# Adding x in the output stage by an accumulating transfer, behind a copy by ScalarE

## The chip, the cores and the metric

The kernel runs on one core of a Trainium2 chip. The metric is the time of one execution on the device in microseconds (us); three runs of the kernel before stand for its time. Engines are named as in the profile: PE is TensorE's matrix multiplication and PEld its weight load, DVE is VectorE, ACT is ScalarE, POOL is GpSimd, SP is SyncE. A name with a q is that engine's sequencer, which also issues transfers (SPq, POOLq).

## The reference

One layer of a trunk: an RMS norm, a pooling mixer whose branch is gated, a residual addition and a final RMS norm, on x of 4096 rows and 1024 columns in float32.

```python
normed = rms_norm(x, norm_w)
u, gate = split(normed @ in_w, 2)               # 1024 -> 2048
pooled = trailing means of u over 2/4/8/16 rows - u
y = (pooled @ group_w + group_b) * scale * silu(gate)
h = x + y @ out_w                               # the output stage: 1024 -> 1024
out = rms_norm(h, final_w)
```

## The kernel before

The products are done in float32 with two parts: a number is split into a rounded high part and a rest (`split`, L167 to L170: ScalarE copies the high part, VectorE subtracts for the rest), and each product is three matmuls (`mm3`). On top of that every large product is cut into 2 x 2 quarters and done with seven products, P1 to P7, in place of eight (a Strassen-Winograd scheme).

There are three stages in the list `steps` (L1069): "a" and "b" compute the gate and the pooled branch in blocks of 1024 rows and store the gated branch as `yd`; "o", the output stage, multiplies it by out_w, adds x and normalizes. The output stage starts near 615 us of the span and takes 8 blocks of 512 rows.

A block of the output stage has 256 rows in "half 1" (the first ones) and 256 in "half 0". Each half is held as two row tiles j = 0 and 1 of 128 rows and 1024 columns, `hs[b][half, j]`, and each row tile has two column halves n = 0 and 1 of 512. The order of the products is P1, P7, P6, P2, P5, P4, P3 (`ORDER_OUT`). Four pairs of PSUM banks rotate from block to block: x, v, y and spare. What is done behind each product, in `evict_o`:

- P1 fills the pair x, and ScalarE copies it into y as the start of P6 (L1023).
- P7 fills v; it is added into half 1, n = 1. P6 adds to y; y is added into half 1, n = 0.
- P2 adds to x; x is added into half 0, n = 0.
- P5 adds to y; y is added into half 1, n = 1. P4 adds to v; v is added into half 1, n = 0; half 1 is complete, and `finish` normalizes and stores it.
- P3 adds to y; y is added into half 0, n = 1; half 0 is complete.

All these additions are VectorE's (L1033), of 128 x 512 from a bank, into row tiles that hold x already: `load_h` (L852) takes a row tile and lets SyncE load x into it, 512 KB each, four products ahead of use.

From block 2 on, P2 is itself cut into seven inner products of half the size ("inner blocks"). P2, P3 and P4 go to the banks x[0] and x[1], P1 and P7 to spare[0] and spare[1] (`product_inner`, L701). `add_inner` (L711) adds 128 columns of a spare bank into a row tile of half 0. The inner P6 and P5 add on to spare[0] during and after the outer P5:

```python
            if j == 1 and inner and i == P5:     # between the two rows of the outer P5
                product_inner(P6)
                add_inner(0, (1, 0))
                add_inner(1, (1, 0), (1, 1))
...
        elif inner and i == P5:                  # behind the outer P5
            product_inner(P5)
            add_inner(0, (0, 1), (1, 1))
```

So spare[0] is read three times, and each inner product that adds on to it has to wait until the reading before it is done. `add_inner(0, (0, 0))`, the first reading, stands at the head of P2's eviction (L1013).

The order of instructions on an engine follows the program, except where the framework's scheduler takes one that is ready earlier; each engine then works its list in that order, and waits are semaphores that the framework sets from the tiles that an instruction reads and writes. A transfer waits on the queue of the engine that issues it. Transfers of the output stage are all on SyncE (x, yd, out); GpSimd only does the small arithmetic of the inverse root in `finish` (L207 to L225).

## Time and profile before

| | us |
|---|---|
| median of 3 runs | 911.19 (911.1 to 911.32) |
| span of the profiled execution, first to last instruction | 909.7 |
| PE busy | 900.6 |
| DVE busy | 764.5 |
| ACT busy | 461.8 |
| POOL busy | 49.9 |

The page gives no time of the profiled execution beside its span; the median of the runs is 1.5 us longer. In rows of a timeline the columns are start, duration, engine, line, operation, written tile <- read tile, shapes and count; brackets hold the idle time of the engine before the row and what ended it. In rows of groups the figures behind the bar are busy time, mean duration in ns, and idle time with its releasers.

### The profile page before, as it was taken

To read this page: it belongs to the slowest core of one execution; us is meant where nothing else is said; L and a number is where in the kernel's file an instruction comes from. 1 tells how busy PE (TensorE), PEld (TensorE's weight loads), DVE (VectorE), ACT (ScalarE), POOL (GpSimd) and SP (SyncE) were. 2 spreads that over 40 slices of the span, in tenths; PEclk is the share of its full clock that TensorE was granted. 3 is DMA by queue.
4 is the path that set the end of the run, shared out by engine and by line. 5 is a ranking of instruction groups with operands and counts; after the bars stand their busy time and mean duration, and the time that the engine had idled before them with its cause. 6 is when DMAs were issued, how large, how long until landed. Compare 5 with 4: busy or idle time off the path is not lost.

```text
span 909.7 us, 11455 instructions
## 1 busy us (share of the span) xinstructions
PE 900.6 (99%) x4320; PEld 790.1 (87%) x4320; DVE 764.5 (84%) x909; ACT 461.8 (51%) x693; POOL 49.9 (5%) x124
## 2 busy tenths in 40 slices
PE   9999999999999999999999999999999999999997
PEld 7888888888888888888888888888888898888886
DVE  3889995985995997696798699699989878978886
ACT  7869547547446565355445545644424424335334
POOL 0020100100110000000000000000201001001000
PEclk9999999999999999999999999999999999999998
DMA  9977766577675454116616714636385464464332
GB/s 341 401 291 240 276 235 230 189 270 253 217 272 196 156 202 145 47 64 212 255 47 234 275 70 158 235 105 219 137 280 181 149 226 155 146 232 139 116 139 93
DMA packets 66807, 178.08 MB, mean 196 GB/s; under 512 B 6080, under 2 KB 23872, under 8 KB 66752
## 3 DMA queue, kind: packets, MB, share of 16 engines
q1 hardware_dynamic: 60176, 155.83, 48.8%
q0 software_dynamic: 5856, 20.46, 6.1%
q10 hardware_dynamic: 720, 1.06, 0.3%
q8 instruction: 34, 0.56, 0.2%
q14 instruction: 21, 0.17, 0.1%
HBM read 116.50 MB, written 60.83 MB: 195 GB/s over the span
## 4 chain that ended last, share of the span: by engine, by line
PE 91%; DMA 4%; DVE 3%; issue 1%; ACT 0%; SPq 0%; POOL 0%; DVEq 0%; ACTq 0%; POOLq 0%
PE bank L603 88%; PE bank L701 3%; DMA early<-in_wut 2%; DMA st<-in_x 1%; DMA vt<-yd 1%; DVE vt L1033 1%; PE bank L406 1%; DVE op L159 1%; DVE st L159 0%; DVE vt L916 0%; ACT st L943 0%; DVE vt L162 0%; DVE vt L711 0%; SPq L370 0%; DVE st L1033 0%
## 5 line engine op out<-in xcount | busy, mean ns | idle before, releaser
L603 PE MATMUL bank<-op,w 128*128 128x512 f32 x2688 | 580.9, 379 | 0.0
L603 PEld LDWEIGHTS bank<-op,w 128*128 128x128 f32 x2688 | 508.5, 189 | 71.8 <-ACT bank L165 0.4
L603 PE MATMUL bank<-w,op 128*128 128x512 f32 (+1 forms) x1212 | 262.2, 377 | 0.0
L603 PEld LDWEIGHTS bank<-w,op 128*128 128x128 f32 x1212 | 226.3, 189 | 30.7
L165 ACT ACTIVATE op<-st 128x1024 fp32r<-128x1024 f32 x129 | 134.7, 1053 | 142.2 <-PE bank L603 90.5
L159 DVE TENSOR_TENSOR op<-st,op 128x1024 fp32r<-128x1024 f32 x129 | 156.8, 1222 | 51.7 <-ACT op L165 51.3
L156 DVE TENSOR_TENSOR vt<-vt 128x1024 f32<-128x1024 f32 (+6 forms) x72 | 88.2, 1236 | 0.6
L159 DVE TENSOR_TENSOR op<-vt,op 128x1024 fp32r<-128x1024 f32 x43 | 52.5, 1222 | 19.8 <-ACT op L165 19.6
L165 ACT ACTIVATE vt<-bank 128x512 f32<-128x512 f32 x82 | 47.6, 593 | 41.4 <-PE bank L603 40.5
L165 ACT ACTIVATE op<-vt 128x1024 fp32r<-128x1024 f32 x43 | 45.1, 1053 | 39.3 <-PE bank L603 30.2
L159 DVE TENSOR_TENSOR st<-st,st 128x1024 f32<-128x1024 f32 (+1 forms) x43 | 47.0, 1111 | 2.3 <-ACT st L912 1.3
L165 ACT ACTIVATE bank<-bank 128x512 f32<-128x512 f32 x48 | 27.9, 581 | 32.9 <-PE bank L603 32.9
L1033 DVE TENSOR_TENSOR vt<-bank,vt 128x512 f32<-128x512 f32 (+1 forms) x55 | 37.1, 677 | 7.4 <-PE bank L603 7.0
L165 ACT ACTIVATE st<-bank 128x512 f32<-128x512 f32 x48 | 27.8, 593 | 28.7 <-PE bank L603 22.3
L207 POOL TENSOR_SCALAR oms<-oss 128x2 f32<-128x2 f32 x14 | 8.4, 601 | 565.5 <-ACT st L912 460.6
L159 DVE TENSOR_TENSOR w<-st,w 128x1024 fp32r<-128x1024 f32 x25 | 30.2, 1223 | 7.8 <-ACT w L165 7.8
L165 ACT ACTIVATE w<-st 128x1024 fp32r<-128x1024 f32 x25 | 26.0, 1052 | 14.2 <-PE bank L603 9.6
L788 DVE SCALAR_TENSOR_TENSOR st<-vt,colt,st 128x512 f32<-128x512 f32 x46 | 32.7, 752 | 0.1
L1033 DVE TENSOR_TENSOR st<-bank,st 128x512 f32<-128x512 f32 x42 | 28.8, 692 | 3.9 <-PE bank L603 3.7
L783 DVE SCALAR_TENSOR_TENSOR vt<-vt,vt 128x1024 f32<-128x1024 f32 x24 | 29.4, 1227 | 0.3
L916 DVE SCALAR_TENSOR_TENSOR vt<-vt,ors,st 128x1024 f32<-128x1024 f32 x18 | 22.5, 1282 | 7.9 <-POOL ors L225 7.9
L165 ACT ACTIVATE st<-st 128x1024 f32<-128x1024 f32 x16 | 16.9, 1059 | 21.8 <-DVE st L156 21.7
(132 smaller groups left out, 619.0 us busy)
## 6 DMA issues: line engine op xcount, KB each, us to landing
st<-in_x SPq DMA_DIRECT2D x30, 512.0 KB, 5.3
st<-in_xt SPq DMA_DIRECT2D x28, 512.0 KB, 5.6
sd<-st POOLq DMA_DIRECT2D x28, 512.0 KB, 4.6
vt<-in_x SPq DMA_DIRECT2D x27, 512.0 KB, 4.5
st<-sd SPq DMA_DIRECT2D x24, 512.0 KB, 4.2
yd<-st SPq DMA_DIRECT2D x23, 512.0 KB, 2.6
st<-yd SPq DMA_DIRECT2D x20, 512.0 KB, 4.6
out<-vt SPq DMA_DIRECT2D x18, 512.0 KB, 3.6
```

Source lines behind the costliest of these rows:

```text
L156: nc.vector.tensor_tensor(out=dst, in0=a, in1=b, op=ALU.add)
L159: return nc.vector.tensor_tensor(out=dst, in0=a, in1=b, op=ALU.subtract)
L165: return nc.scalar.activation(dst, src, func)
L207: (nc.vector if on_vector and not first else nc.gpsimd).tensor_scalar(out=ms, in0=ss, scalar1=1.0 / D, scalar2=EPS, op0=ALU.mult, op1=ALU.add)
L406: latest[0] = nc.tensor.matmul(ps, a[:, kk, 2 * j + t, :], maps, start=t + m == 0, stop=t == 1 and m == len(pairs) - 1,).ins
L603: latest[0] = nc.tensor.matmul(ps, a, b, start=start and n == 0, stop=stop and n == 2, skip_group_check=True).ins
L701: latest[0] = nc.tensor.matmul(ps, x1, x2, start=i in (P1, P7) and k + n == 0, stop=k == 1 and n == 2, skip_group_check=True,).ins
L783: nc.vector.scalar_tensor_tensor(out=s[:, :, at : at + H], in0=s[:, :, at : at + H], scalar=1.0 / win, in1=v[:, :, HIST:], op0=ALU.mult, o ...
L788: nc.vector.scalar_tensor_tensor(out=sg[:, j], in0=s[:, j, at : at + H], scalar=bias_c[2 * grp + j], in1=sg[:, j], op0=ALU.add, op1=ALU.mult,)
L916: nc.vector.scalar_tensor_tensor(out=us[j], in0=us[j], scalar=rs[:, j : j + 1], in1=fw[0], op0=ALU.mult, op1=ALU.mult,)
L1033: partial["added"] = nc.vector.tensor_tensor(out=dst, in0=src, in1=dst, op=ALU.add).ins
```

## The change

In blocks 0 to 6 the first bank that goes to a part of a row tile (P7, P6, P2) is no longer added to x by VectorE; ScalarE copies it, and x is added to the row tile behind it by a transfer on GpSimd's queue that accumulates into SBUF. Half 1 gets x for all columns behind P6, half 0 for the left columns behind P2; the right columns of half 0 (P3) are still loaded ahead by SyncE, 256 KB a row tile, and added by VectorE. `add_inner(0, (0, 0))` moves behind P2's copies. The last block loads and adds as before.

```diff
     def load_h(b, half):
         for j in range(2):
             u = take("p (a b) -> p a b", a=2)
-            r = b * TO + (1 - half) * TH + j * P
-            nc.sync.dma_start(out=u.rearrange("p a b -> p (a b)"), in_=x[r : r + P, :])
+            if b == NBO - 1:
+                nc.sync.dma_start(
+                    out=u.rearrange("p a b -> p (a b)"), in_=x[row_of(b, half, j), :]
+                )
+            elif half == 0:
+                nc.sync.dma_start(out=u[:, 1], in_=x[row_of(b, half, j), H:])
             hs[b][half, j] = u
+
+    def add_h(b, half, cols):
+
+        for j in range(2):
+            u = hs[b][half, j].rearrange("p a b -> p (a b)")
+            nc.gpsimd.dma_start(
+                out=u[:, cols], in_=x[row_of(b, half, j), cols], accum_op=ALU.add
+            )
...
         if inner and i == P2:
             inner["rows"] = [hs[b][0, j][:, 0] for j in range(2)]
-            add_inner(0, (0, 0))
...
             u = hs[b][half, j][:, n]
+            if not final and i in (P7, P6, P2):
+                copy(halved(u), plain(ps[j]))
+                continue
             last = final and i in (P4, P3)
...
+        if inner and i == P2:
+            add_inner(0, (0, 0))
+        if not final and i == P6:
+            add_h(b, 1, slice(0, D))
+        elif not final and i == P2:
+            add_h(b, 0, slice(0, H))
         if final and i == P3:
```

## The prediction

> **What bounds the kernel now.** The page comes first, for the span and the engines' shares.

> ```profile
> span 909.7 us, 11455 instructions
> PE 900.6 (99%) x4320; PEld 790.1 (87%) x4320; DVE 764.5 (84%) x909; ACT 461.8 (51%) x693; POOL 49.9 (5%) x124
> PE 91%; DMA 4%; DVE 3%; issue 1%; ACT 0%; SPq 0%; POOL 0%; DVEq 0%; ACTq 0%; POOLq 0%
> ```

> TensorE is busy for 99% and holds 91% of the chain that ended last. The runs shown have a median of 911.19 us, so 1.5 us lie around the span; the sums below are changes to the span, and I add them to the median. Next the stage that is changed, by the table of windows (columns: PE, PEld, DVE, ACT, POOL busy, granted clock, DMA share, GB/s).

> ```profile
> 700.00:740.00 40.00, 40.00 (x212) 35.65 (x211) 35.10 (x47) 15.49 (x21) 1.93 (x10) 1.00 0.67 228
> 740.00:780.00 40.00, 40.00 (x217) 35.93 (x216) 34.20 (x44) 15.38 (x21) 3.30 (x10) 1.00 0.40 141
> 820.00:860.00 40.00, 39.74 (x207) 35.16 (x206) 33.97 (x46) 16.18 (x22) 3.02 (x10) 1.00 0.42 145
> ```

> TensorE has no idle time in two of them and 0.26 us in the third, at clock 1.00. VectorE is at 85 to 88%, ScalarE at 39%. Taking work from VectorE can therefore win only what TensorE loses to VectorE. Since a busy PE can hide short waits, I looked for them in the timeline of each inner block (2 to 6), at the weight loads.

> ```profile
> 708.84 0.75 PEld L701 LDWEIGHTS bank<-inner,op 128*128 128x128 f32 x6 [0.19 <-DVE vt L711]
> ...
> 780.52 0.74 PEld L701 LDWEIGHTS bank<-inner,op 128*128 128x128 f32 x6 [0.28 <-DVE vt L711]
> ...
> 849.79 0.68 DVE L1033 TENSOR_TENSOR st<-bank,st 128x512 f32<-128x512 f32 x1
> ...
> 851.52 0.69 DVE L1033 TENSOR_TENSOR vt<-bank,vt 128x512 f32<-128x512 f32 x1
> ...
> 852.12 0.42 DVE L711 TENSOR_TENSOR vt<-bank,vt 128x256 f32<-128x256 f32 x1
> 852.59 0.74 PEld L701 LDWEIGHTS bank<-inner,op 128*128 128x128 f32 x6 [0.67 <-DVE vt L711]
> ```

> In blocks 2, 4 and 6 the inner P6 writes spare bank 0 before VectorE has read it in `add_inner(0, (0, 0))`. The three waits make 0.19 + 0.28 + 0.67 = 1.14 us. The tail holds nothing for this change:

> ```profile
> 889.30 2.61 PE bank L603 x12
> 891.93 0.69 DVE vt L1033
> ```

> VectorE takes up the chain at 891.93 right behind a matmul of the last block, so it arrives there without a backlog, and the last block is unchanged.

> **The change part by part.** It touches blocks 0 to 6.

> ```profile
> L165 ACT ACTIVATE st<-bank 128x512 f32<-128x512 f32 x48 | 27.8, 593 | 28.7 <-PE bank L603 22.3
> ...
> L1033 DVE TENSOR_TENSOR vt<-bank,vt 128x512 f32<-128x512 f32 x53 | 36.2, 687 | 7.4 <-PE bank L603 7.0
> ```

> *Removed from VectorE:* 6 additions a block at 0.687 us, 4.1 us a block, 28.9 us in all. *Added to ScalarE:* 6 copies a block at 0.593 us, 3.6 us a block; its 15.4 of 40 us becomes about 19.4. Both lie beside TensorE. On the path they are worth at most the 1.14 us. In block 6, two additions that go (849.79 and 851.52, 0.6 us of the stream each) stand shortly before the 852.12 one, so it starts about 1.2 us earlier against a wait of 0.67; blocks 2 and 4 waited less. I take the whole 1.14 us.

> *Loads on SyncE:* four x loads of 512 KB a block become two of 256 KB (right half of half 0). The view of SyncE's waits shows what they held up:

> ```profile
> SPq L856 <- DVE op L159: 37.6, 11, 7.9
> ```

> For 37.6 us the queue stood at such a load until a slot was free. Fewer loads waiting for a slot let the yd loads behind them go earlier. No such landing ends a TensorE wait except through the 0.67 already counted, so I book nothing. The wait for a free slot moves to ScalarE's first copy; the x load into the same slot used to be issued long before that point, so I price it at nothing too.

> *Added to GpSimd:* four accumulating transfers a block, two of 512 KB behind P6 and two of 256 KB behind P2. No accumulating transfer is in this trace. The nearest rows are this queue's plain ones, from the views of the lines L515 (512 KB out of SBUF) and L492 (256 KB into SBUF):

> ```profile
> L515 POOL DMA_DIRECT2D sd<-st x25: 531/537/554, 53.2 to 269.2; - x25
> ...
> DMA to landing us min/median/max: 2.9/3.8/12.2
> ```
> ```profile
> L492 POOL DMA_DIRECT2D vt<-rd x6: 556/556/558, 87.8 to 242.4; - x6
> ...
> DMA to landing us min/median/max: 3.4/3.8/6.1
> ```

> An issue holds GpSimd for 0.54 us; landing takes 3.8 us, at least 2.9 and at most 12.2. Is GpSimd free when it is needed?

> ```profile
> 756.84 0.70 POOL L207 TENSOR_SCALAR oms<-oss 128x2 f32<-128x2 f32 x1 [28.82 <-ACT st L912]
> ```

> It is: ahead of the RMS chain of block 3 it had idled 28.82 us, through P7, P6, P2 and P5.

> *The new wait.* VectorE's later additions into the same rows now stand behind these transfers. Block 3, one without a wait, gives the times:

> ```profile
> 738.78 1.50 PE L701 MATMUL bank<-w,op 128*128 128x256 f32 x12
> 738.98 0.69 DVE L1033 TENSOR_TENSOR vt<-bank,vt 128x512 f32<-128x512 f32 x1 [1.06 <-PE bank L603]
> ...
> 740.11 0.83 PE L701 MATMUL bank<-inner,op 128*128 128x256 f32 x6
> ...
> 741.65 0.42 DVE L711 TENSOR_TENSOR vt<-bank,vt 128x256 f32<-128x256 f32 x1
> ...
> 744.72 0.83 PE L701 MATMUL bank<-inner,op 128*128 128x256 f32 x6
> 744.92 0.69 DVE L1033 TENSOR_TENSOR st<-bank,st 128x512 f32<-128x512 f32 x1 [0.98 <-PE bank L603]
> ...
> 745.38 2.76 PE L603 MATMUL bank<-w,op 128*128 128x512 f32 x12
> ...
> 745.58 1.22 DVE L711 TENSOR_TENSOR vt<-bank,vt 128x256 f32<-128x256 f32 x3
> ...
> 747.98 0.83 PE L701 MATMUL bank<-inner,op 128*128 128x256 f32 x6
> 748.18 0.69 DVE L1033 TENSOR_TENSOR vt<-bank,vt 128x512 f32<-128x512 f32 x1 [1.38 <-PE bank L603]
> ...
> 749.82 1.23 DVE L159 TENSOR_TENSOR op<-st,op 128x1024 fp32r<-128x1024 f32 x1 [0.22 <-ACT op L165]
> ```

> Half 1: P6 ends at 738.78. ScalarE copies its second bank by about 740.5 at the latest (one split of 1.06 us may stand ahead), and the transfer is issued by 741. P5's eviction of that row stands at 748.18, a budget of 7 us, and only VectorE waits there: the next split behind it (749.82) is for P1 of the next block, which starts behind P4 and P3, 48 matmuls of 2.61 / 12 = 0.217 us, at 748.8 + 10.4 = 759.2 (749.82 + 1.23 leaves 8 us). It costs nothing up to a landing of some 15 us.

> Half 0 is the tight one. P4's inner product fills bank x1 by 740.94; ScalarE's copy ends at 741.53. Row 1's transfer can start then, or, if row 0's is issued first, behind the addition of 741.65 (ends 742.07) and one issue, at 742.7. Row 1 is read by the first of the three additions that stood at 745.58, 0.42 us each, and the inner P5 at 747.98 must not write spare bank 0 before it. So row 1 must have landed by about 747.5: a budget of 4.8 to 5.9 us. Queued behind that addition are the two of bank 1, P5's second eviction, two more L711 and the split with 8 us to spare; only the inner P5 is urgent, in the 5 inner blocks 2 to 6. Below the price of a copy nothing can be gained, since TensorE is full. At 3.8 us there is no stall; at 6.1 it is 6.1 - 4.8 = 1.3 us a block, 6.5 us; at 12.2 it is 7.4 a block, 37 us. I take 3.8, the 256 KB row, which has this size, this queue and this direction, and keep the rest for the range. It leaves 1.0 to 2.1 us of cover; what lands later than that is paid five times.

> [...] The queue's plain transfers moved their bytes at this rate:

> ```profile
> q0 software_dynamic: 5856, 20.46, 6.1%
> ```

> 6.1% of 909.7 us is 55.5 us for 20.46 MB, 0.71 us for 256 KB and 1.42 us for 512 KB. [...]

> *Moved:* `add_inner(0, (0, 0))` now comes behind both copies in the program; it still needs only row 0's copy (0.593 us from 740.3) and P1's inner product, and has until 744.7. In the last block it may fall behind one addition of 0.687 us, again inside that room.

> **Sum.** 911.19 - 1.14 = 910.05; some tenths may come back where one row lands late. Forecast **910.3 us**.

> **Rivals.** *Row 1 lands late (slower).* One mechanism at one place: the addition for half 0, row 1 waits for its transfer, spare bank 0 isn't read, the inner P5 stands. It decides from a landing of 4.8 to 5.9 us. With the slowest 256 KB row (6.1): 910.05 + 6.5 = 916.6. For it: 12.2 was seen for a 512 KB transfer, and the DMA share reaches 0.67 here. Against it: the median of 3.8, and less SyncE traffic. [...] *ScalarE is late with P6's copies:* P5 needs bank y1 read by 745.38, and the copy is done by 740.5 even behind a split; a Square waiting on VectorE ahead of it would have to cost 5 us. If that happens once a block at 0.6 us beyond the room, 910.05 + 5 x 0.6 = 913. *The additions are relieved but the three waits stay*, because VectorE's order or the yd load sets them: 911.2. *More is won than 1.14 us:* 909 or less; nothing in the windows speaks for it.

> **Chances.** A measurement of this kernel can tell about 0.2%, 1.8 us, from no change (909.4 to 913.0 count as the same). Forecast, with the case that the waits stay: 0.47. Doubled row: 0.15, half of it within 0.2%. Row 1 late by over that: 0.27, and much later (towards 12.2): 0.05. ScalarE late: 0.02, slower. More won: 0.04. Same 0.47 + 0.07 = 0.54; slower 0.08 + 0.27 + 0.05 + 0.02 = 0.42; faster 0.04. The range runs from 909.6 to 924.0 (a landing of 4.8 + 14/5 = 7.6 us); some 0.15 stays outside. The likeliest sign's own range is 909.6 to 912.9.

> **What the profile after would show.** No L603 or L701 row with an idle time put down to VectorE at the inner P6 says the 1.14 us were won. If the inner P5 has idle weight loads in blocks 2 to 6, with the L711 ahead of it waiting for a transfer from x, the late row is it. [...] VectorE's busy time should fall by 29 us and ScalarE's rise by 25. The prediction is wrong if accumulating is far slower than a plain load, or if the schedule puts row 1's issue or its addition elsewhere.

## The result and the profile after

The changed kernel takes **926.3 us** in the median of four runs (922.87 to 929.25), the kernel before 911.26 beside it (911.1 to 911.33): a ratio of 1.0162 with an interval of 1.0145 to 1.0179. Forecast was no change, 910.3 us, with 924.0 as the upper end. It is slower by 15 us. The profiled execution took 927.64 us around its span of 925.9.

The page of the changed kernel, in the parts that answer to those shown of before (engines, queue, three groups):

```profile
span 925.9 us, 11551 instructions
PE 907.0 (98%) x4320; PEld 793.9 (86%) x4320; DVE 739.6 (80%) x867; ACT 484.9 (52%) x735; POOL 70.9 (8%) x152
...
q0 software_dynamic: 9888, 31.47, 12.6%
...
L701 PE MATMUL bank<-inner,op 128*128 128x256 f32 x144 | 22.3, 295 | 10.7 <-DVE vt L711 10.7
...
L701 PEld LDWEIGHTS bank<-inner,op 128*128 128x128 f32 x144 | 20.0, 205 | 13.0 <-DVE vt L711 12.7
L711 DVE TENSOR_TENSOR vt<-bank,vt 128x256 f32<-128x256 f32 x36 | 14.1, 419 | 19.6 <-DMA vt<-in_x 17.0
```

Work moved between the engines much as worked out: VectorE lost 24.9 us (28.9 forecast; 24.9 / 42 is 0.59 us an addition, its time in a row of them, where a single row lasts 0.687), ScalarE gained 23.1 (25 forecast). But weight loads of the inner products (L701) now idle for 12.7 us behind `add_inner` (L711), and that idles for 17.0 us behind transfers out of x. The packets of the queue q0, GpSimd's, take 12.6% of the 16 DMA engines' span where they took 6.1%.

The windows of the stage, same columns as before (PE, PEld, DVE, ACT, POOL, granted clock, DMA share, GB/s):

```profile
700.00:740.00 40.00, 36.21 (x176) 31.72 (x176) 28.04 (x36) 16.23 (x25) 5.50 (x14) 0.91 0.65 184
740.00:780.00 40.00, 40.00 (x207) 35.34 (x206) 28.82 (x37) 19.18 (x29) 7.75 (x15) 1.00 0.60 163
```

In the first, TensorE has lost 3.8 us, and the clock, 1.00 before, is 0.91 in the mean. In the second (block 3) nothing is lost. The timeline of block 2 shows the place:

```profile
701.97 1.50 PE L701 MATMUL bank<-w,op 128*128 128x256 f32 x12
...
703.91 0.88 POOL L867 DMA_DIRECT2D st<-in_x  x1 [2.41 <-ACT st L165]
...
705.18 0.87 POOL L867 DMA_DIRECT2D vt<-in_x  x1 [0.39 <-ACT vt L165]
...
709.93 0.88 POOL L867 DMA_DIRECT2D vt<-in_x  x1 [3.89 <-issue]
...
714.64 1.22 DVE L711 TENSOR_TENSOR vt<-bank,vt 128x256 f32<-128x256 f32 x3 [4.23 <-DMA vt<-in_x]
715.12 1.35 PEld L701 LDWEIGHTS bank<-inner,op 128*128 128x128 f32 x6 [4.19 <-DVE vt L711]
```

Read from below: the inner P5 (715.12) has waited 4.19 us for VectorE to read spare bank 0. The three additions at 714.64 waited 4.23 us for a transfer from x: that of 705.18, half 0's row 1, issued ahead of row 0's (709.93). Its issue held GpSimd for 0.87 us. The inner P5 of the other four inner blocks waited like this:

```profile
753.72 0.74 PEld L701 LDWEIGHTS bank<-inner,op 128*128 128x128 f32 x6 [0.34 <-DVE vt L711]
...
791.99 1.21 PEld L701 LDWEIGHTS bank<-inner,op 128*128 128x128 f32 x6 [2.63 <-DVE vt L711]
...
831.21 0.74 PEld L701 LDWEIGHTS bank<-inner,op 128*128 128x128 f32 x6 [1.92 <-DVE vt L711]
...
870.42 1.14 PEld L701 LDWEIGHTS bank<-inner,op 128*128 128x128 f32 x6 [3.57 <-DVE vt L711]
```

The view of line L867, cut to a single issue, gives its landing. Here are the second transfer of half 1 and, next in the queue, row 1, in block 2 and then in block 3:

```profile
L867 POOL DMA_DIRECT2D st<-in_x x1: 882/882/882, 703.9 to 703.9; - x1
...
DMA to landing us min/median/max: 9.3/9.3/9.3
...
L867 POOL DMA_DIRECT2D vt<-in_x x1: 866/866/866, 705.2 to 705.2; - x1
...
DMA to landing us min/median/max: 9.4/9.4/9.4
...
L867 POOL DMA_DIRECT2D vt<-in_x x1: 885/885/885, 746.4 to 746.4; - x1
...
DMA to landing us min/median/max: 5.4/5.4/5.4
...
L867 POOL DMA_DIRECT2D vt<-in_x x1: 875/875/875, 747.6 to 747.6; - x1
...
DMA to landing us min/median/max: 5.5/5.5/5.5
```

In both blocks row 1 lands 1.3 to 1.4 us behind half 1's last transfer (703.9 + 9.3 = 713.2 and 705.2 + 9.4 = 714.6; 751.8 and 753.1), in all five inner blocks 1.2 to 2.5 us behind it, as on a queue that works in order. From block 2 to 6 row 1 takes 9.4, 5.5, 7.8, 7.1 and 8.8 us. Each less the wait behind it leaves 5.2 us: that is the room, inside the 4.8 to 5.9 us that the prediction gave it.

Why the five differ shows in the windows from half 1's first issue to row 1's landing, here of blocks 2 and 3:

```profile
700.60:714.60 14.00, 10.73 (x68) 9.55 (x66) 7.66 (x8) 4.81 (x6) 3.53 (x4) 0.97 0.95 225
743.10:753.10 10.00, 10.00 (x65) 9.25 (x64) 3.57 (x4) 3.76 (x5) 3.54 (x4) 1.00 0.94 167
```

The DMA engines are busy throughout: 0.95, 0.94, 0.94, 0.95 and 1.03 in blocks 2 to 6. They move 225, 167, 210, 186 and 261 GB/s there; GpSimd's bytes are about the same in each, so the rest is SyncE's. Row 1 lands soonest (5.5 us) where SyncE moves least and latest (9.4 and 8.8) where it moves most; no run changed SyncE's traffic alone.

The other part of the loss is the clock. The windows that follow are cut on the points where it changes:

```profile
710.27:713.68 3.41, 1.06 (x5) 0.58 (x4) 0.14 (x1) 1.06 (x1) 0.55 (x1) 1.00 1.06 191
713.68:717.09 3.41, 1.97 (x8) 1.88 (x9) 2.06 (x5) 0.50 (x1) 0.00 (x0) 0.50 0.18 31
717.09:720.50 3.41, 3.41 (x10) 2.69 (x9) 2.74 (x4) 0.56 (x1) 0.00 (x0) 0.50 0.14 30
720.50:723.91 3.41, 3.41 (x17) 2.98 (x16) 1.84 (x3) 1.33 (x3) 0.00 (x0) 1.00 0.38 126
788.77:792.19 3.42, 1.19 (x6) 0.73 (x5) 0.65 (x2) 1.06 (x1) 0.00 (x0) 1.00 0.62 130
792.19:795.60 3.41, 3.41 (x12) 2.96 (x12) 3.20 (x7) 1.06 (x1) 0.00 (x0) 0.50 0.00 0
829.73:833.15 3.42, 1.93 (x12) 1.80 (x13) 2.41 (x6) 1.95 (x2) 0.00 (x0) 1.00 0.34 60
867.28:870.69 3.41, 0.27 (x2) 0.27 (x3) 0.71 (x2) 0.90 (x1) 0.00 (x0) 1.00 0.69 162
870.69:874.10 3.41, 3.41 (x12) 2.96 (x12) 3.27 (x7) 1.06 (x1) 0.00 (x0) 0.50 0.00 0
```

Behind three of the waits the granted clock is 0.50 for whole stretches of 3.41 us: 10 matmuls fit into 717.09:720.50, 17 into the next stretch of the same length at 1.00. TensorE is busy there, so this loss is in no idle column. Half of the busy time in the four halved stretches, (1.97 + 3 x 3.41) / 2, is 6.1 us.

**The sum.** 910.05 + 12.7 of waits + 6.1 of half clock = 928.9, against 927.64 for this execution. The 12.7 are the waits of the weight loads; the multiplications, which still have work when the next weight load begins to wait, idle for 10.7 there, and with these the sum is 926.9. So it holds to about 1 us. One difference lies ahead of block 2's waits: its P2 begins at 701.97, where the same row of the kernel before is

```profile
702.95 1.50 PE L701 MATMUL bank<-w,op 128*128 128x256 f32 x12
```

1.0 us later. Why is open.

### The profile page after: what moved, and what is told of

It is laid out like the page before. It is cut to its first block, busy times and chain, and to the rows that moved or that the text cites. A ratio compares the mean times of both kernels' runs of the same rounds, so it can differ in the third digit from the quotient of the medians.

```text
span 925.9 us, 11551 instructions
## 1 busy us (share of the span) xinstructions
PE 907.0 (98%) x4320; PEld 793.9 (86%) x4320; DVE 739.6 (80%) x867; ACT 484.9 (52%) x735; POOL 70.9 (8%) x152
## 3 DMA queue, kind: packets, MB, share of 16 engines
q0 software_dynamic: 9888, 31.47, 12.6%
q10 hardware_dynamic: 720, 1.06, 0.3%
## 5 line engine op out<-in xcount | busy, mean ns | idle before, releaser
L603 PE MATMUL bank<-op,w 128*128 128x512 f32 x2688 | 580.9, 379 | 0.0
L603 PEld LDWEIGHTS bank<-op,w 128*128 128x128 f32 x2688 | 507.9, 189 | 72.4 <-ACT bank L165 0.4
L603 PE MATMUL bank<-w,op 128*128 128x512 f32 (+1 forms) x1212 | 266.5, 381 | 0.0
L603 PEld LDWEIGHTS bank<-w,op 128*128 128x128 f32 x1212 | 229.4, 192 | 32.2
L159 DVE TENSOR_TENSOR op<-st,op 128x1024 fp32r<-128x1024 f32 x129 | 156.3, 1219 | 64.5 <-ACT op L165 64.1
L165 ACT ACTIVATE op<-st 128x1024 fp32r<-128x1024 f32 x129 | 135.0, 1052 | 137.9 <-PE bank L603 81.9
L165 ACT ACTIVATE vt<-bank 128x512 f32<-128x512 f32 x105 | 61.3, 594 | 46.6 <-PE bank L603 46.2
L159 DVE TENSOR_TENSOR op<-vt,op 128x1024 fp32r<-128x1024 f32 x43 | 52.3, 1219 | 21.5 <-ACT op L165 21.4
L165 ACT ACTIVATE op<-vt 128x1024 fp32r<-128x1024 f32 x43 | 45.1, 1053 | 33.1 <-PE bank L603 26.3
L165 ACT ACTIVATE st<-bank 128x512 f32<-128x512 f32 x67 | 38.9, 591 | 34.8 <-PE bank L603 22.9
L159 DVE TENSOR_TENSOR st<-st,st 128x1024 f32<-128x1024 f32 (+1 forms) x43 | 46.9, 1108 | 2.7 <-ACT st L924 1.3
L165 ACT ACTIVATE bank<-bank 128x512 f32<-128x512 f32 x48 | 27.9, 580 | 32.6 <-PE bank L603 32.5
L867 POOL DMA_DIRECT2D st<-in_x x10 | 8.9, 891 | 388.8 <-ACT st L165 378.4
L159 DVE TENSOR_TENSOR w<-st,w 128x1024 fp32r<-128x1024 f32 x25 | 30.1, 1216 | 7.9 <-ACT w L165 7.9
L165 ACT ACTIVATE w<-st 128x1024 fp32r<-128x1024 f32 x25 | 26.0, 1052 | 14.6 <-PE bank L603 9.7
L701 PE MATMUL bank<-inner,op 128*128 128x256 f32 x144 | 22.3, 295 | 10.7 <-DVE vt L711 10.7
L701 PEld LDWEIGHTS bank<-inner,op 128*128 128x128 f32 x144 | 20.0, 205 | 13.0 <-DVE vt L711 12.7
L711 DVE TENSOR_TENSOR vt<-bank,vt 128x256 f32<-128x256 f32 x36 | 14.1, 419 | 19.6 <-DMA vt<-in_x 17.0
```

Of the source, the lines that this page charges most:

```text
L159: return nc.vector.tensor_tensor(out=dst, in0=a, in1=b, op=ALU.subtract)
L165: return nc.scalar.activation(dst, src, func)
L603: latest[0] = nc.tensor.matmul(ps, a, b, start=start and n == 0, stop=stop and n == 2, skip_group_check=True).ins
L701: latest[0] = nc.tensor.matmul(ps, x1, x2, start=i in (P1, P7) and k + n == 0, stop=k == 1 and n == 2, skip_group_check=True,).ins
L711: nc.vector.tensor_tensor(out=dst, in0=src, in1=dst, op=ALU.add)
L867: nc.gpsimd.dma_start(out=u[:, cols], in_=x[row_of(b, half, j), cols], accum_op=ALU.add)
```

## The experiments

The theory: row 1's transfer lands late, because an accumulating transfer takes longer, and because half 1's, 1 MB, stands ahead of it on the same queue. The rivals: something else in the change (ScalarE's copies, GpSimd's issues, the moved addition) holds the products up; and, for the clock, that the transfers themselves lower it and not the waits. In what follows, the groups and waits of L711 and L701 are the ones to watch.

### Half 1 alone

```diff
-            if b == NBO - 1:
+            if b == NBO - 1 or half == 0:
                 nc.sync.dma_start(
...
-            elif half == 0:
-                nc.sync.dma_start(out=u[:, 1], in_=x[row_of(b, half, j), H:])
...
-            if not final and i in (P7, P6, P2):
+            if not final and i in (P7, P6):
...
-        elif not final and i == P2:
-            add_h(b, 0, slice(0, H))
```

> Only half 1 is changed (copies behind P7 and P6, accumulating transfers of 512 KB behind P6); half 0 is loaded ahead and added by VectorE as before. Theory (late row: the inner P5 stands until VectorE has added into half 0, row 1, whose accumulating transfer lands 5.5 to 9.4 us after its issue in the changed kernel): no weight load at the inner P5 waits for L711, granted clock 1.00 up to the tail, 910.0 to 911.5 us. Rival (the copies on ScalarE or the accumulating traffic as such cost the time): the 1 MB a block that stays is two thirds of the traffic, so 10 of the 15 us stay, 918 us or more.

910.35 us, ratio 0.999 (0.9981 to 0.9999). A group from the view of the lines:

```profile
L701 PEld LDWEIGHTS bank<-inner,op 128*128 128x128 f32 x144 | 18.9, 192 | 0.6
```

No weight load waits for L711 any more, not at the inner P6 either, where those of before did, and L711 idles for 0.2 us. The time is 0.6 us under the 910.98 of the kernel before beside it. Of half 1 itself, 1 MB of accumulating transfers and four copies a block cost nothing. What is gained lies below the 0.2% that the prediction gave as the least that can be told, so it can't confirm the 1.14 us.

### Half 0 alone

```diff
-            if b == NBO - 1:
+            if b == NBO - 1 or half == 1:
...
-            if not final and i in (P7, P6, P2):
+            if not final and i == P2:
...
-        if not final and i == P6:
-            add_h(b, 1, slice(0, D))
-        elif not final and i == P2:
+        if not final and i == P2:
             add_h(b, 0, slice(0, H))
```

> Only half 0 is changed (copies behind P2, two accumulating transfers of 256 KB); half 1 as before. Theory, with the queue as its cause (row 1 moves only behind half 1's 1 MB on the same queue): row 1 now has the queue to itself and lands 4.0 to 4.8 us after its issue, inside the room of 5.9 us; no wait or tenths, 910.3 to 912.5 us. Rival (an accumulating transfer behind P2 is too slow by itself): landing stays at 5.5 us or above, a wait of 0.5 to 2 us in each of the five blocks, 914 us or more.

912.34 us, ratio 1.001 (1.0001 to 1.002). The view of L867 has both rows of all blocks in one:

```profile
DMA to landing us min/median/max: 3.7/5.3/7.5
```

Row 0's transfer is issued behind row 1's, and only row 1 is urgent. Cut to row 1, the view gives 5.2, 3.7, 3.8, 7.3 and 3.8 us in blocks 2 to 6; block 6 is

```profile
L867 POOL DMA_DIRECT2D vt<-in_x x1: 915/915/915, 850.3 to 850.3; - x1
...
DMA to landing us min/median/max: 3.8/3.8/3.8
```

So an accumulating row with nothing ahead of it lands in three blocks of five as soon as the prediction took, 3.8 us, and sooner than the 4.0 to 4.8 expected here. One wait of note is left, in block 5. The timeline at that place, and the window around it:

```profile
820.40 0.74 PEld L701 LDWEIGHTS bank<-inner,op 128*128 128x128 f32 x6 [2.16 <-DVE vt L711]
```
```profile
816.00:822.00 6.00, 4.24 (x23) 3.50 (x22) 4.04 (x7) 1.79 (x2) 0.00 (x0) 1.00 0.89 230
```

There the DMA engines are busy for 0.89 of the time with other queues' transfers too, and the rows take 7.3 and 7.5 us. So most of the loss needs half 1 ahead in the queue; in block 5, with none of it ahead, row 1 is late beside that traffic.

### Row 1 of half 0 as before, all else changed

```diff
-            if not final and i in (P7, P6, P2):
+            if not final and (i in (P7, P6) or i == P2 and j == 0):
...
-            if b == NBO - 1:
+            if b == NBO - 1 or half == 0 and j == 1:
...
-        for j in range(2):
+        for j in range(1 + half):
             u = hs[b][half, j].rearrange("p a b -> p (a b)")
             nc.gpsimd.dma_start(
```

> The changed kernel, but half 0, row 1 is loaded ahead and added by VectorE as before; row 0 and half 1 stay accumulated. Theory (row 1 is the only urgent one): the inner P5 no longer waits; row 0 lands about 12 us after P2's start, VectorE waits some 3 us for it behind the inner P5, inside the 8 us of cover: 910.3 to 912 us. Rival (the wait moves on to row 0's next addition and from there through the splits behind it to TensorE): 915 us or more.

910.0 us, ratio 0.9989 (0.9981 to 0.9998). The view of the lines, and that of L867:

```profile
L701 PEld LDWEIGHTS bank<-inner,op 128*128 128x128 f32 x144 | 18.8, 191 | 0.7
...
L711 DVE TENSOR_TENSOR vt<-bank,vt 128x256 f32<-128x256 f32 x36 | 14.1, 419 | 2.1 <-DMA vt<-in_x 1.8
```
```profile
DMA to landing us min/median/max: 5.0/7.2/9.3
```

The transfers land as slowly as in the changed kernel, yet no product waits: the loss hangs on the one tile, row 1 of half 0, that must be there by the inner P5. VectorE waits for row 0 only 1.8 us in all. Of the versions tried this is the fastest, 0.1% under the kernel before, less than the 0.2% that a single comparison was said to tell.

### A plain load in place of the accumulating one

```diff
-                out=u[:, cols], in_=x[row_of(b, half, j), cols], accum_op=ALU.add
+                out=u[:, cols], in_=x[row_of(b, half, j), cols]
```

> The changed kernel with plain transfers of the same bytes on the same queue in place of the accumulating ones, so that x replaces the products copied before (it leaves out the sum of those parts). Theory (a row takes 328 ns per 4 KB where a copied one takes 159): row 1 lands about 4 us after its issue, no or short waits, 910.3 to 913 us. Rival (it is the queue's issue path on GpSimd and the order behind half 1, not the accumulation): landings of 5.5 us and more stay, 918 us or more.

This kernel leaves out the sum, since x replaces the copied products. 910.28 us, ratio 0.9992 (0.9983 to 1.0001), with the same bytes, the same number of issues and half 1 ahead as before. The view of L867, and the queue on its page:

```profile
L867 POOL DMA_DIRECT2D vt<-in_x x18: 537/551/608, 636.6 to 850.0; - x18
...
DMA to landing us min/median/max: 2.9/4.8/7.2
```
```profile
q0 software_dynamic: 8992, 31.47, 9.6%
```

The issue takes 0.55 us where the changed kernel's take 0.87. Less the 55.5 us of before, the queue's time here is 9.6% of 908.3, 87.2 - 55.5 = 31.7 us for 11.01 MB, 2.9 us a MB; in the changed kernel 12.6% of 925.9, 116.7 - 55.5 = 61.2 us for the same bytes, 5.6 us a MB. That is 1.9 times, and 2.05 times the 2.71 us a MB (55.5 / 20.46) of the kernel before. Row 1 lands after 5.6, 3.7, 4.8, 3.8 and 5.4 us in blocks 2 to 6 here, and all that is left of the waits at the inner P5 is 0.44 and 0.22 us, where it passes the room of 5.2. So row 1 is late by two things together: half 1's bytes ahead of it, and their accumulation, which about doubles the time that they take. With plain bytes ahead (here), or with nothing ahead (half 0 alone), it is nearly always in time.

### Only the left columns of half 1

```diff
-            if not final and i in (P7, P6, P2):
+            if not final and i in (P6, P2):
...
-            elif half == 0:
+            else:
                 nc.sync.dma_start(out=u[:, 1], in_=x[row_of(b, half, j), H:])
...
-            add_h(b, 1, slice(0, D))
+            add_h(b, 1, slice(0, H))
```

> The changed kernel, but of half 1 only the left columns (P6) are copied and accumulated, 256 KB a row tile; its right columns (P7) are loaded ahead and added by VectorE as before. Theory (row 1 of half 0 lands late because the queue works in order and half 1's rows, at 328 ns per 4 KB, stand ahead of it): 1.3 us less per transfer ahead, so row 1 lands up to 2.6 us earlier; of the waits of 4.2, 0.3, 2.6, 1.9 and 3.5 us some 1 to 3 us in all remain, and the clock is seldom halved: 911.5 to 915 us. Rival (the landing of row 1 depends on its own transfer and on other queues' traffic alone): waits and time as in the changed kernel, 922 us or more.

914.92 us, ratio 1.0045 (1.0029 to 1.0061). Its waits at the inner P5:

```profile
PEld bank L701 <- DVE vt L711: 4.9, 5, 1.7
```

Halving the bytes that stand ahead takes the waits from 12.7 to 4.9 us (more was left than expected), and with the longest at 1.7 us the clock stays at 1.00 up to the end. Row 1 lands after 6.9, 5.4, 6.8, 6.1 and 5.7 us; less the room of 5.2 this is 1.7, 0.2, 1.6, 0.9 and 0.5, the five waits, 4.9 in all. The time agrees within 0.7 us: 910.05 + 4.9 = 914.95, against 914.24 for this execution. One rival stays untested: whether row 1 waits for its turn on GpSimd's queue or only for its share of full DMA engines. No run sent half 1's transfers over another queue.

### Waits without transfers

To see whether waits alone halve the clock, I held spare bank 0 in the kernel before by multiplications of it by 1.0 on VectorE (0.427 us each), so that the inner P5 has to wait. `HOLD` gives the count by block.

```diff
                 product_inner(P6)
+                for _ in range(HOLD.get(hold_b[0], 0)):
+                    spare = plain(sets_bank(0))[:, :, 0:P]
+                    nc.vector.tensor_scalar(
+                        out=spare, in0=spare, scalar1=1.0, scalar2=None, op0=ALU.mult
+                    )
                 add_inner(0, (1, 0))
...
+    HOLD, hold_b = {2: 6, 3: 9, 4: 12, 5: 15, 6: 18}, [0]
     partial = {}
...
+            hold_b[0] = b
             product_out(i, split_up.pop(n), sets, n == len(steps) - 1)
```

> The kernel before, without accumulating transfers; behind the inner P6 VectorE first multiplies the used columns of spare bank 0 by 1.0 in place, 6, 9, 12, 15 and 18 times in blocks 2 to 6, so that the inner P5 waits a set time. By the additions' 0.34 us each in the stream the waits are about 0.3, 1.3, 2.3, 3.3 and 4.4 us. Theory (a wait of more than some 2 us at the inner P5 is by itself what halves the granted clock behind it, for one or two stretches of 3.4 us): no halving in blocks 2 and 3, one stretch in 4 or 5, one or two in 6, and 927 to 929 us. Rival (the halving goes with the accumulating transfers): clock 1.00 up to the tail, 922 to 923 us.

> As the kernel with the held bank, with the counts in reverse order (18, 15, 12, 9, 6 in blocks 2 to 6). Theory: the halved stretches move with the long waits, to blocks 2 and 3 (4 perhaps), none in 5 and 6. Rival (they belong to places in the program): they stay in the late blocks.

> The kernel before with the bank held in blocks 3 and 5 alone, 14 and 20 times, so that VectorE can catch up in between and the inner P5 waits longer than in the two kernels with five holds, whose waits stayed under 1.7 us (granted clock 1.00). Theory (a long wait by itself halves the clock behind it): waits of 3 us or more, and a stretch of 3.4 us or two at clock 0.5 behind each. Rival (the halving goes with accumulating transfers): waits of the same length with clock 1.00 up to the tail.

These missed. With 6 to 18 operations from block 2 to 6: 916.14 us, ratio 1.0058 (1.004 to 1.0076), no wait over 1.4 us. With 18 to 6: 914.69 us (one run), none over 1.7 in its profile. With 14 and 20 in blocks 3 and 5: 917.59, ratio 1.0072 (1.0054 to 1.009), one of 2.2 us. The clock was not halved in any of the profiled executions. The scheduler puts other products' matmuls ahead of the inner P5 where that would wait (in block 3 of the last one 46 of L603 lie between the inner P6 and P5, where the kernel before has 12), so the waits stayed far below those expected. Next I kept P4's matmuls behind the inner P5:

```diff
-            product_out(i, split_up.pop(n), sets, n == len(steps) - 1)
+            hold_b[0] = b
+            pinned = i == P4 and b in HOLD
+            with tc.issue_after(latest[0]) if pinned else nullcontext():
+                product_out(i, split_up.pop(n), sets, n == len(steps) - 1)
```

> The kernel before with the bank held 11 and 16 times in blocks 3 and 5, and the matmuls of P4 kept behind the inner P5 in these blocks: without that the scheduler had put them ahead of it, so that TensorE hardly waited. Waits of about 2.9 and 5.1 us. Theory (idle time of TensorE is by itself what halves the granted clock): at least the longer wait is followed by a stretch of 3.4 us at 0.5; 919 to 924 us. Rival (it goes with accumulating transfers): clock 1.00 up to the tail, 918 to 919.5 us.

> The same with 16 holds each in blocks 2, 4 and 6: three waits of about 5 us. Theory (idle time alone): stretches at 0.5 behind most of them, as the changed kernel had behind 4.2, 2.6 and 3.5 us; 926 to 934 us. Rival (accumulating transfers): clock 1.00 up to the tail, 925 to 926 us.

The waits were shorter than expected again, since still other products went ahead. 11 and 16 operations in blocks 3 and 5: 916.24 us, ratio 1.0061 (1.0046 to 1.0076), with waits of 0.26 and 2.10 us. 16 in blocks 2, 4 and 6: 918.51, ratio 1.0082 (1.0065 to 1.0099), none over 1.7 and the clock not halved. But the one wait of 2.10 us did it (timeline and windows of the first of these two):

```profile
833.45 0.84 PEld L701 LDWEIGHTS bank<-inner,op 128*128 128x128 f32 x6 [2.10 <-DVE vt L711]
```
```profile
830.64:834.06 3.42, 1.51 (x13) 1.29 (x12) 3.21 (x8) 1.06 (x1) 0.00 (x0) 1.00 0.00 0
834.06:837.47 3.41, 3.41 (x11) 2.77 (x11) 3.03 (x6) 1.06 (x1) 0.00 (x0) 0.50 0.00 0
```

No accumulating transfer is in this kernel, and the DMA share is 0.00 there. So accumulating transfers are not needed for the clock to fall; a wait is enough. This rests on one wait in one execution.

### The changed kernel again

> The changed kernel once more, for its waits and its clock. Both theories of the waits: the inner P5 waits in most of blocks 2 to 6, 923 to 929 us. On the clock: waits over 2.5 us are followed by stretches of 3.4 us at 0.5, waits under 2 us are not.

923.87 us (one run). Waits of 3.91, 0.36, 3.05, 0.93 and 3.43 us, 11.7 in all. The waits came as expected. The clock did not: of the three waits over 2.5 us only the last is followed by a half clock. Here the windows at the first and the last:

```profile
711.05:714.46 3.41, 1.78 (x9) 1.22 (x7) 0.00 (x0) 1.06 (x1) 0.00 (x0) 1.00 1.08 208
714.46:717.88 3.42, 1.54 (x10) 1.47 (x11) 1.99 (x5) 0.68 (x1) 0.00 (x0) 1.00 0.42 75
717.88:721.29 3.41, 3.41 (x18) 2.98 (x17) 3.41 (x6) 0.38 (x2) 0.00 (x0) 1.00 0.15 36
864.65:868.06 3.41, 1.41 (x9) 1.35 (x10) 1.85 (x5) 0.55 (x1) 0.00 (x0) 1.00 0.48 100
868.06:871.47 3.41, 3.41 (x9) 2.70 (x8) 2.85 (x4) 0.51 (x1) 0.00 (x0) 0.50 0.00 0
```

910.05 + 11.7 + 3.41 / 2 = 923.5, against 923.87, with one halved stretch in place of four; with the 9.7 us that the multiplications idle it is 921.5. So the sum holds to 2.4 us or better. The spread of the changed kernel (922.87 to 929.25) fits: part of it is how many waits are followed by a half clock. The mean clocks of its four runs are 0.996, 0.994, 0.990 and 0.991 in the order of their times (922.87, 924.95, 927.64 and 929.25), so the clock is not all of it.

## Why the prediction was wrong, point by point

- **What bounds the kernel, and the 1.14 us:** the mechanism was right, the size can't be told. TensorE is the bound (busy for 99% of the span before and 98% after), and the waits at the inner P6 go. Half 1 alone, and all but row 1, measured 910.35 and 910.0, which is 0.6 and 1.0 us under the kernel before beside them (910.98). The 1.14 are waits of weight loads; the multiplications of L701 idled for only 0.3 us in the kernel before.
- **The new wait's place and room:** right. It is the inner P5 behind L711, in all five inner blocks, with 5.2 us of room.
- **The step that failed: "I take 3.8, the 256 KB row, which has this size, this queue and this direction".** Row 1 landed after 5.5 to 9.4 us, past its room of 5.2 in all five blocks. For a row with nothing ahead 3.8 was right: half 0 alone had it in three blocks of five. But in the changed kernel half 1's 1.05 MB are issued shortly before, and the sum put no time for them. By the 5.6 us a MB that the accumulating transfers take they are 5.9 us of queue ahead of row 1 (an estimate), where plain ones, at 2.9, would be 3.0. Taking half of the bytes away left 4.9 of the 12.7 us of waits, taking all away left one wait above 1 us (2.2), and making them plain brought the time back to 910.28. The row's own accumulation (0.7 us of queue more) and its issue (0.87 us in place of 0.54) are the smaller parts.
- **Half 1 "costs nothing up to a landing of some 15 us":** right for those who read half 1, as its run alone shows. But it priced the transfer by its own readers only. What it costs is paid by the next one on the queue. SyncE's traffic, with which row 1's landing rose from block to block, the prediction named only as a doubt (the DMA share of 0.67).
- **The doubled row, at 0.15 of the chances, and 912.9 as the end of the likeliest sign's range:** no run shows this price. What the runs showed in its place: a MB of accumulating transfers took 5.6 us of the queue, 2.05 times the 2.71 of the plain ones in the kernel before (why is open), and the changed kernel took 926.3 us, 13.4 more than 912.9. At 5.6 us a MB, what P6 and P2 put on the queue is 1.57 MB, 8.8 us a block.
- **The rivals.** "Row 1 lands late" is what happened, at 0.27, with its landing taken as 6.1 where the median of the five is 7.8. ScalarE was not late, and the waits did not stay.
- **A term that stood nowhere:** the clock, 6.1 us in the profiled execution. Each wait was priced at its own length. The waits alone would have made 910.05 + 12.7 = 922.8 us, still under the upper end of 924.0: the late row moved the time, and the clock took it out of the range.

## What to carry to other kernels

Price a transfer by its queue, not by its size: add up what was issued ahead of it on the same queue, at the rate of that kind of transfer, and look at what other queues move at that time, before asking whether its reader has room. If a kind of transfer isn't in the trace, take the price of its nearest plain relative as a lower bound (here it was half), and a change that hangs on it should give the tight reader (here one row tile of four) its data in another way. And look for a wait's cost behind it too: here, with TensorE otherwise full, five waits that left 1.91 to 3.14 us idle within one stretch of 3.41 us were each followed by half clock, at an estimated 1.7 us (half of 3.41) for each full stretch of it, on top of their length.

## What the runs showed of the hardware

```profile
836.08:839.50 3.42, 1.50 (x10) 1.20 (x8) 3.42 (x8) 1.06 (x1) 0.00 (x0) 1.00 0.83 261
```

So in these runs the border lies near 1.9 us of a cell of 3.41, and a wait's position on the grid counted beside its length: in the second run 3.91 and 3.05 us, split over two cells each (1.63 and 1.88, 1.18 and 1.47), did nothing, and in the pinned kernel 2.10 us, 1.91 of it within one cell, did. The whole executions of the changed kernel and of the kernel before, each cut on the grid on which its own clock changes, from 30 us on, the end included, sort the same way: at a clock of 1.00 every cell with 2.09 us idle or more was followed by a half clock (the one of 2.09 is the last at 1.00 of the kernel before), and none with 1.49 or less; no cell lay between. The cell of 713.68, itself at half clock and with only 1.44 us idle, was followed by another half clock; why is open. This sorting was read after the fact; no run moved a wait on the grid on purpose.

Row 0's issue in block 2 came 3.89 us after GpSimd was free, which held up nothing. It began at 709.93, and half 1's first transfer, issued at 700.59, landed 9.0 us later, at 709.6. The same distance of 0.3 us lies between that landing and row 0's issue in all five inner blocks. So the fourth accumulating transfer of a block was not issued before the first had landed. With plain transfers it was: 705.8 there, 2.0 us ahead of the first one's landing at 707.8. What holds it back is open, and so is why P2 of block 2 began 1 us earlier.
